# Down products reading their operand at other addresses, and an up product in halves of 256 columns

## The chip, the cores and the metric

The kernel runs on one core of one Trainium2 chip. The metric is the device time of one execution in microseconds. Matrix products run on TensorE (PE in the rows; PEld is its weight load), the rest on VectorE (DVE), ScalarE (ACT) and GpSimd (POOL); SyncE (SP) issues the weights' DMAs.

## The reference

Two layers on a sequence of 512 tokens of width 1024. Layer 1 mixes with a convolution and a recurrence, layer 2 with sliding-window attention. Each layer ends in the same feed-forward block, and that block is all that the change touches:

```
def conv_glu_ffn(x, norm_g, w_up, conv_w, conv_b, w_down):      # D_FF = 2816
    h = rms_norm(x, norm_g)
    u = h @ w_up                                                # [512,1024] @ [1024,5632]
    gate = causal_dwconv(u[..., :D_FF], conv_w, conv_b)         # 3 taps
    return (jax.nn.silu(gate) * u[..., D_FF:]) @ w_down         # [512,2816] @ [2816,1024]
```

## The kernel before, in words

Everything lies feature-major: 128 features on the partitions, the 512 tokens as columns. A product of float32 exactness is made of three products of rounded halves (type float32r): weights and operand are each split into a high and a low part, and for each 128x128 block of weights TensorE does high weights by high operand, high by low, low by high. That is `gemm` (lines 167 to 178). Each of the three is one MATMUL of 128x512 with a weight load of 128x128 of its own in front of it, so the high weights are loaded twice.

`wpieces` and `wparts` (lines 143 to 164) bring the weights: a raw piece of 128x1024 by one DMA on SP's queue (two buffers), of which ScalarE casts one half at a time to `whi` (line 150) and VectorE subtracts to `wlo` (line 151). `whi` and `wlo` have three buffers each (WHL = 3). One such half feeds two output blocks by two blocks of depth, so 12 MATMULs.

`ffn` (line 680) runs eleven rounds over pairs of feature blocks. A round has two up products: `pg` for the gate and `pu` for the other factor, 48 MATMULs each, with `xgh` and `xgl` as the moving operand. Then VectorE scales the gate (`gp`, line 707), ScalarE and VectorE apply the taps (lines 709 and 712), ScalarE the silu, VectorE multiplies by `pu` (line 715), and the result is split into row f of `hh` and `hl` (lines 183 and 184). After the rounds the down product reads `hh` and `hl` as its moving operand: eight output blocks by 22 blocks of depth by 3 parts, 528 MATMULs. The order of the instructions on each engine is written by the program's scheduler from the dependences; TensorE takes its MATMULs in the order in which they stand.

Where the operands lie in a partition (bytes, from the built program of before; all rows of an operand are 2048 bytes apart, all blocks of weights 512 bytes):

```
operand                  first byte          the same modulo 512   product that reads it
whi, wlo (all buffers)   78912 ... 89152      64                   every product (weights)
xgh, xgl                 37952, 54336         64                   up products, keys, queries
oh, ol                   139904, 156288      128                   attention's output (lines 174, bank)
mc, mr                   121280, 137664      448                   mixer's output (lines 174, bank)
hh, hl (both layers)     104800, 149856      352                   down products
```

The attention's value product (line 866) is the one place where a float32r product already streams 256 columns at a time: there `xgh` or `xgl` is the loaded operand (128x128) and `whi` or `wlo` the moving one, as two runs of 128 columns, 2048 bytes apart.

Of the kernel before, what the change touches and what calls it, by code (L numbers as in the profile page):

```python
# [11 lines left out]
F32 = mybir.dt.float32  # L12
F32R = mybir.dt.float32r
# [4 lines left out]
DRAM = bass.MemoryType.DRAM  # L18

P = 128  # L20
T = 512
D = 1024
# [12 lines left out]
FC = DFF // P  # L35
# [21 lines left out]
# vectors of the features, in columns of 128: widths in columns, first columns  # L57
# [11 lines left out]
class Net:  # L69
# [17 lines left out]
    # activations that share a table set, in the order of the sets  # L87
# [17 lines left out]
    # banks: rings of one pool; those of the large products in turn, those of everything else in turn  # L105
# [60 lines left out]
    # m blocks of the product, over the blocks kb..ke of its depth; xh, xl start at block kb  # L166
    def gemm(self, w, b0, xh, xl, m=2, kb=0, ke=None, pss=None, first=True, last=True, prep=None):
        ke = w.shape[2] if ke is None else ke
        pss = pss or [self.pmm() for _ in range(m)]
        for k0, kn, hi, lo in self.wpieces(w, b0, m, kb, ke, prep):  # L170
            for i, ps in enumerate(pss):
                for k in range(kn):
                    kk = k0 + k - kb
                    mm = lambda a, b, **kw: self.nc.tensor.matmul(ps, lhsT=a[:, i, k, :], rhs=b[:, kk, :], **kw)  # L174
                    mm(hi, xh, start=first and kk == 0, stop=False)
                    mm(hi, xl, start=False, stop=False)
                    mm(lo, xh, start=False, stop=last and k0 + k == ke - 1)
        return pss
# [12 lines left out]
    # rs = rsqrt(-2 * ps + eps), ps = -0.5 * mean square  # L191
# [14 lines left out]
    # residual stream -> gained and split operand of the next product, and its rms factor  # L206
# [48 lines left out]
    def mixer(self):  # L255
        nc, tc, ap = self.nc, self.tc, self.ap
        V, S, G = nc.vector, nc.scalar, nc.gpsimd
# [5 lines left out]
        with ExitStack() as es:  # L263
# [70 lines left out]
            # mt: rows (S | k), columns (a t | r t); mbt: b rows (r t), and the transposed inverses;  # L334
            # bkt, sv: token-major (b | k) decayed to the chunk end, and (S | v)
# [21 lines left out]
            def keys(fc):  # L357
# [4 lines left out]
                # normalised key (negated)  # L362
# [30 lines left out]
                # in-chunk matrices, transposed: rows (b s | k s), columns (a t | r t)  # L393
# [15 lines left out]
                # the corner between the two diagonal blocks waits in the room of the states  # L409
                S.copy(sv[0:LH, fc, :, :, 0:LH], mt[0:LH, :, :, LH:L])  # L410
                S.copy(mbt[0:64, fc], mt[0:64, :, :, L:P])
                # the rows of b have left; the chunk-start features take their place
                for eo in range(2):
                    G.dma_start(mt[0:64, eo], ar[eo * 64 : eo * 64 + 64])
                # bonus: the decays of r and of k cancel
# [12 lines left out]
            def values(fc):  # L428
                bk, ep = bks[fc], eps[fc]
                v = shift(self.gemm(win, 16 + fc, xh, xl, m=1)[0], 8 + fc, "v")  # L430
                V.tensor_tensor(out=bv[:, fc, :], in0=bv[:, fc, :], in1=v, op=ALU.mult)
                # token-major b, k (decayed to the chunk end) and v
                for c in range(NCH):
                    S.activation(out=bk[:, c, :], in_=bk[:, c, :], func=AF.Identity, scale=ep[:, c, L : L + 1])
                for c0 in range(0, NCH, 4):
                    p4 = self.psum().rearrange("p (c t) -> p c t", t=P)
                    for c in range(4):
                        nc.tensor.transpose(out=p4[:, c, :], in_=bk[:, c0 + c, :], identity=self.ident)
                    S.copy(bkt[:, fc, :, c0 : c0 + 4, :].rearrange("p e c n -> p c e n"), p4.rearrange("p c (e n) -> p c e n", e=2))
                    p4 = self.psum().rearrange("p (c t) -> p c t", t=P)  # L440
                    for c in range(4):
                        cc = c0 + c
                        if cc == 0:
                            nc.tensor.matmul(p4[64:128, c, :], lhsT=v[:, 0:L], rhs=self.ident, start=True, stop=True)
                        else:
                            nc.tensor.transpose(out=p4[:, c, :], in_=v[:, (cc - 1) * L : (cc + 1) * L], identity=self.ident)
                    S.copy(sv[64:128, fc, :, c0 : c0 + 4, :].rearrange("p e c n -> p c e n"),
                           p4[64:128].rearrange("p c (e n) -> p c e n", e=2))

# [81 lines left out]
            for c in range(NCH):  # L531
                for g in range(2):
# [8 lines left out]
                    # four products are open at once in this bank: products with zeros open and close them all  # L541
# [12 lines left out]
                    # the updates take the place of the state  # L554
# [124 lines left out]
    def ffn(self, l, out=None, aside=None):  # L679
# [7 lines left out]
        with ExitStack() as es:  # L687
# [3 lines left out]
            hh = big.tile([P, FC, T], F32R, name="hh")  # L691
            hl = big.tile([P, FC, T], F32R, name="hl")
            rstd = big.tile([P, T], F32, name="rstd")
            for fp in range(FC // 2):
                if fp == 2 and aside:
                    aside()
                pg = self.gemm(wu, 2 * fp, xh, xl)
                if fp == 0:
                    self.table("natural_log_exp_and_others")
                    self.rms_rows(tr, "t2", rstd, ln=True)  # L700
                    self.table("silu_and_others")
                pu = self.gemm(wu, FC + 2 * fp, xh, xl)
                for i in range(2):
                    f = 2 * fp + i
                    gp = tr.tile([P, 2 + T], F32, tag="gp", name="gp")
                    G.memset(gp[:, 0:2], 0.0)  # L706
                    V.tensor_tensor(out=gp[:, 2:], in0=pg[i], in1=rstd, op=ALU.mult)  # L707
                    t = tr.tile([P, T], F32, tag="t2", name="t", bufs=T3)
                    S.activation(out=t, in_=gp[:, 2:], func=AF.Identity, scale=self.pc("ffn_conv_w", (3 * l + 2) * FC + f),  # L709
                                 bias=self.pc("ffn_conv_b", l * FC + f))  # L710
                    for j in (1, 0):
                        V.scalar_tensor_tensor(out=t, in0=gp[:, j : j + T], scalar=self.pc("ffn_conv_w", (3 * l + j) * FC + f), in1=t,  # L712
                                               op0=ALU.mult, op1=ALU.add)
                    self.fn(out=t, in_=t, func=AF.Silu)
                    V.tensor_tensor(out=t, in0=t, in1=pu[i], op=ALU.mult)  # L715
                    self.split(hh[:, f, :], hl[:, f, :], t)
            for b0 in range(0, DC, 2):
                for i, ps in enumerate(self.gemm(wd, b0, hh, hl)):
                    m = b0 + i
# [76 lines left out]
    def attention(self):  # L796
# [10 lines left out]
        with ExitStack() as es:  # L807
# [24 lines left out]
            # keys: normalised, rotated, on both halves of the partitions  # L832
# [25 lines left out]
            # values, token-major  # L858
# [14 lines left out]
            # queries: biased, gained, rotated; the rms factor waits for the scores  # L873
# [3 lines left out]
            def queries(j):  # L877
# [9 lines left out]
                # -(rms factor) / 8  # L887
# [14 lines left out]
            def block(m, b):  # L902
# [8 lines left out]
                # row tiles of the tensor engine run side by side: even and odd heads on two banks  # L911
# [21 lines left out]
                for kb in range(nkb):  # L933
# [3 lines left out]
                    # even heads first  # L937
# [39 lines left out]
def _blocks(w):  # L977
    # [K, M] -> [M / 128, 128 (row in block), K / 128, 128 (column in block)]
    k, m = w.shape
    return w.reshape(k // P, P, m // P, P).transpose(2, 1, 0, 3)  # L980


def _columns(inputs):
# [5 lines left out]
    # conv taps: rows (tap mod 4, channel mod 32), columns (channel / 32, tap / 4)  # L989
# [40 lines left out]
```

## Time and profile before

| | us |
|---|---|
| three timed executions | 1236.13, 1236.25, 1239.99 |
| median | 1236.25 |
| span of the profiled execution, first to last instruction | 1235.5 |
| TensorE busy | 1216.2 (98% of the span), 6231 MATMULs, 6231 weight loads |
| VectorE, ScalarE busy | 717.7 (58%), 551.1 (45%) |
| granted TensorE clock, mean | 0.999 |
| layer 1: up product, down product (from, to) | 359.7 to 555.7 (last nine rounds), 555.7 to 678.9 |
| layer 2: up product, down product (from, to) | 867.1 to 1107.3, 1107.3 to 1230.2 |

The profile gives no time of the profiled execution beside its span; the span lies 0.75 us under the median of the timed runs. A MATMUL's length in the profile is from its start until its result is out, and consecutive ones overlap. What a MATMUL costs in a stream is the distance from its start to the next one's start.

### The profile page before, as it was taken

Reading aid. Unit: us, or ns where it says so; the run is one execution under the profiler, and the core shown is the slowest. Engines: PE = TensorE matmul, PEld = TensorE weight load, DVE = VectorE, ACT = ScalarE, POOL = GpSimd, SP = SyncE. Lnnn points to the kernel's source line nnn. Section 1 sums busy time; section 2 is a strip of 40 time slices with the busy share of each in tenths; the row PEclk is TensorE's granted clock in tenths of the full one; section 3 lists DMA queues with packets and bytes.
Section 4 is the critical chain, followed back from the end, with each engine's and each line's share of the span. In section 5 each row is a group of like instructions: output and inputs, shape, how many; then the busy total and the mean of one; then the engine's idle time right before and its main releaser. Section 6 shows DMA issues by size and latency. Waiting matters only on the chain.

```text
span 1235.5 us, 16559 instructions
## 1 busy us (share of the span) xinstructions
PE 1216.2 (98%) x6231; PEld 948.3 (77%) x6231; DVE 717.7 (58%) x1360; ACT 551.1 (45%) x1031; POOL 72.0 (6%) x210
## 2 busy tenths in 40 slices
PE   7999999999999999999999999999999999999998
PEld 5687875568788888888888876658888888888886
DVE  6797947367766555553333678866655455553332
ACT  6967333365534343342222657764544343432221
POOL 4101031000100000000000030100000000000000
PEclk9999999999999999999999999999999999999999
DMA  6235382022323322323333230102223223233331
GB/s 188 57 90 128 94 196 59 1 86 93 96 98 102 103 88 101 102 87 95 94 95 97 85 103 25 55 20 100 89 99 102 93 96 103 94 94 111 111 111 60
DMA packets 65088, 114.42 MB, mean 93 GB/s; under 512 B 15681, under 2 KB 17937, under 8 KB 65009
## 3 DMA queue, kind: packets, MB, share of 16 engines
q1 hardware_dynamic: 60048, 102.25, 26.9%
q0 software_dynamic: 4816, 10.89, 3.5%
q8 instruction: 49, 0.80, 0.3%
q14 instruction: 31, 0.25, 0.1%
q10 hardware_dynamic: 144, 0.23, 0.1%
HBM read 105.40 MB, written 4.26 MB: 89 GB/s over the span
## 4 chain that ended last, share of the span: by engine, by line
PE 93%; DVE 3%; ACT 2%; DMA 2%; issue 1%; SPq 0%; ACTq 0%; DVEq 0%
PE mm L174 66%; PE bank L174 11%; PE mm L631 2%; PE bank L917 2%; PE bank L942 2%; PE bank L936 1%; PE ps L404 1%; DMA xT<-in_xT_dram 1%; PE ps L538 1%; PE ps L553 1%; PE ps L559 1%; PE bank L885 1%; DMA nb<-nd 1%; PE ps L567 0%; DVE wlo L151 0%
## 5 line engine op out<-in xcount | busy, mean ns | idle before, releaser
L151 DVE TENSOR_TENSOR wlo<-wraw,whi 128x512 fp32r<-128x512 f32 x364 | 250.8, 690 | 360.5 <-ACT whi L150 353.2
L150 ACT CAST whi<-wraw 128x512 fp32r<-128x512 f32 x364 | 224.8, 618 | 431.2 <-PE mm L174 374.9
L174 PE MATMUL mm<-xgh,whi 128*128 128x512 f32 x896 | 351.6, 392 | 9.9 <-ACT whi L150 9.9
L174 PE MATMUL mm<-xgh,wlo 128*128 128x512 f32 x896 | 350.4, 391 | 0.2 <-DVE wlo L151 0.2
L174 PE MATMUL mm<-xgl,whi 128*128 128x512 f32 x896 | 350.2, 391 | 0.0
L174 PEld LDWEIGHTS mm<-xgh,whi 128*128 128x128 f32 x896 | 168.6, 188 | 47.2 <-ACT whi L150 10.1
L174 PEld LDWEIGHTS mm<-xgh,wlo 128*128 128x128 f32 x896 | 168.5, 188 | 37.8 <-issue 1.7
L174 PEld LDWEIGHTS mm<-xgl,whi 128*128 128x128 f32 x896 | 168.6, 188 | 36.1 <-issue 1.2
L174 PE MATMUL mm<-hh,whi 128*128 128x512 f32 x352 | 139.1, 395 | 0.0
L174 PE MATMUL mm<-hh,wlo 128*128 128x512 f32 x352 | 139.0, 395 | 0.0
L174 PE MATMUL mm<-hl,whi 128*128 128x512 f32 x352 | 139.0, 395 | 0.0
L174 PEld LDWEIGHTS mm<-hh,wlo 128*128 128x128 f32 x352 | 66.0, 187 | 16.3
L174 PEld LDWEIGHTS mm<-hl,whi 128*128 128x128 f32 x352 | 66.0, 187 | 16.1
L174 PEld LDWEIGHTS mm<-hh,whi 128*128 128x128 f32 x352 | 66.0, 187 | 16.0
L712 DVE SCALAR_TENSOR_TENSOR t<-gp,col,t 128x512 f32<-128x512 f32 x88 | 63.5, 745 | 0.0
L709 ACT ACTIVATE t<-gp,col 128x512 f32<-128x512 f32 x44 | 35.7, 816 | 35.3 <-DVE gp L707 34.7
L183 ACT CAST hh<-t 128x512 fp32r<-128x512 f32 x44 | 27.3, 622 | 36.9 <-DVE t L715 36.6
L707 DVE TENSOR_TENSOR gp<-mm,rstd 128x512 f32<-128x512 f32 x44 | 30.2, 691 | 17.3 <-PE mm L174 17.2
L715 DVE TENSOR_TENSOR t<-t,mm 128x512 f32<-128x512 f32 x44 | 30.1, 687 | 17.2 <-PE mm L174 17.2
L101 ACT ACTIVATE t<-t 128x512 f32<-128x512 f32 x44 | 27.7, 630 | 20.4 <-DVE t L712 20.3
L706 POOL MEMSET gp<- 128x2 f32 x44 | 4.5, 105 | 512.3 <-DVE t L712 451.5
L922 DVE CUSTOM_DVE_ANT_0 pr<-bank,mask,nsnk 128x256 f32<-128x256 f32 (+1 forms) x64 | 31.3, 502 | 3.8 <-PE bank L917 3.7
(323 smaller groups left out, 1452.9 us busy)
## 6 DMA issues: line engine op xcount, KB each, us to landing
wraw<-in_w_up_dram SPq DMA_DIRECT2D x88, 512.0 KB, 3.5
wraw<-in_w_down_dram SPq DMA_DIRECT2D x40, 512.0 KB, 3.7
wraw<-in_w_in_dram SPq DMA_DIRECT2D x22, 512.0 KB, 3.7
wraw<-in_w_qkv_dram SPq DMA_DIRECT2D x12, 512.0 KB, 3.5
wraw<-in_w_out_dram SPq DMA_DIRECT2D x8, 512.0 KB, 3.6
wraw<-in_w_o_dram SPq DMA_DIRECT2D x8, 512.0 KB, 3.5
st<-cpad POOLq DMA_DIRECT2D x24, 135.0 KB, 4.6
xT<-in_xT_dram SPq DMA_DIRECT2D x4, 512.0 KB, 8.6
```

Of the source, the lines that this page charges most:

```text
L101: ins = self.nc.scalar.activation(**kw)
L150: nc.scalar.copy(hi, src)
L151: nc.vector.tensor_tensor(out=lo, in0=src, in1=hi.bitcast(F32), op=ALU.subtract)
L174: mm = lambda a, b, **kw: self.nc.tensor.matmul(ps, lhsT=a[:, i, k, :], rhs=b[:, kk, :], **kw)
L183: nc.scalar.copy(hi, src)
L631: nc.tensor.matmul(pc[b * 32 : b * 32 + 32, :], lhsT=dg[:, b, g, :], rhs=stk[b][:, 4 * g : 4 * g + T], start=g == 0, stop=g == 7, tile_pos ...
L707: V.tensor_tensor(out=gp[:, 2:], in0=pg[i], in1=rstd, op=ALU.mult)
L709: S.activation(out=t, in_=gp[:, 2:], func=AF.Identity, scale=self.pc("ffn_conv_w", (3 * l + 2) * FC + f), bias=self.pc("ffn_conv_b", l * F ...
L712: V.scalar_tensor_tensor(out=t, in0=gp[:, j : j + T], scalar=self.pc("ffn_conv_w", (3 * l + j) * FC + f), in1=t, op0=ALU.mult, op1=ALU.add)
L715: V.tensor_tensor(out=t, in0=t, in1=pu[i], op=ALU.mult)
L917: nc.tensor.matmul(pscs[e][:, hp, :nk], lhsT=qr[hs, h // 2, bs], rhs=kd[m][hs, k0 : k0 + nk], start=True, stop=True)
L922: V.tensor_tensor_reduce(out=pr_[:, i, :nk], in0=pscs[e][:, hp, :nk], in1=mask[:, 2 * P - nk :], op0=ALU.add, op1=ALU.min, scale=rq[:, b, ...
```

## The change

- `gemm` has a new argument `parts`. With 2, each block's three products are done for columns 0 to 255 first and then for columns 256 to 511, each with a weight load of its own. Layer 2's up products have `parts=2`; all others stay at 1.
- Layer 1: a tile of 224 bytes that nobody uses stands ahead of `hh`. In the built program `hh` and `hl` move from 104800 and 149856 to 105024 and 150080, both 64 modulo 512, as the weights.
- Layer 2: rows of `hh` and `hl` are 2080 bytes apart in place of 2048. They begin at 104800 and 150560, and row k lies at 352 + 32 k and 32 + 32 k modulo 512.
- Comments are dropped, which moves line numbers (174 becomes 176, 712 becomes 719).

```
-    def gemm(self, w, b0, xh, xl, ..., prep=None):
+    def gemm(self, w, b0, xh, xl, ..., prep=None, parts=1):
...
-                    mm = lambda a, b, **kw: self.nc.tensor.matmul(ps, lhsT=a[:, i, k, :], rhs=b[:, kk, :], **kw)
-                    mm(hi, xh, start=first and kk == 0, stop=False)
-                    mm(hi, xl, start=False, stop=False)
-                    mm(lo, xh, start=False, stop=last and k0 + k == ke - 1)
+                    for c in range(parts):
+                        cs = slice(c * T // parts, (c + 1) * T // parts)
+                        mm = lambda a, b, **kw: self.nc.tensor.matmul(ps[:, cs], lhsT=a[:, i, k, :], rhs=b[:, kk, cs], **kw)
+                        mm(hi, xh, start=first and kk == 0 and c == 0, stop=False)
+                        mm(hi, xl, start=False, stop=False)
+                        mm(lo, xh, start=False, stop=last and k0 + k == ke - 1 and c == parts - 1)
...
-            hh = big.tile([P, FC, T], F32R, name="hh")
-            hl = big.tile([P, FC, T], F32R, name="hl")
+            if l == 0:
+                big.tile([P, 56], F32, name="gap")
+                hh = big.tile([P, FC, T], F32R, name="hh")
+                hl = big.tile([P, FC, T], F32R, name="hl")
+            else:
+                hh = big.tile([P, FC, T + 8], F32R, name="hh")[:, :, 0:T]
+                hl = big.tile([P, FC, T + 8], F32R, name="hl")[:, :, 0:T]
...
-                pg = self.gemm(wu, 2 * fp, xh, xl)
+                pg = self.gemm(wu, 2 * fp, xh, xl, parts=1 + l)
...
-                pu = self.gemm(wu, FC + 2 * fp, xh, xl)
+                pu = self.gemm(wu, FC + 2 * fp, xh, xl, parts=1 + l)
```

TensorE, where layer 2's up product begins, before (`mm` is an output bank, `xgh` and `xgl` the operand's parts, `whi` and `wlo` the weights'; the number after a name is its buffer):

```order
L174 MATMUL mm_7386<-xgh_7359,whi_7390 128x512
L174 MATMUL mm_7386<-xgl_7360,whi_7390 128x512
L174 MATMUL mm_7386<-xgh_7359,wlo_7391 128x512
L174 MATMUL mm_7386<-xgh_7359,whi_7390 128x512
L174 MATMUL mm_7386<-xgl_7360,whi_7390 128x512
L174 MATMUL mm_7386<-xgh_7359,wlo_7391 128x512
```

The same place in the changed kernel:

```order
L176 MATMUL mm_7387<-xgh_7360,whi_7391 128x256
L176 MATMUL mm_7387<-xgl_7361,whi_7391 128x256
L176 MATMUL mm_7387<-xgh_7360,wlo_7392 128x256
L176 MATMUL mm_7387<-xgh_7360,whi_7391 128x256
L176 MATMUL mm_7387<-xgl_7361,whi_7391 128x256
L176 MATMUL mm_7387<-xgh_7360,wlo_7392 128x256
L176 MATMUL mm_7387<-xgh_7360,whi_7391 128x256
L176 MATMUL mm_7387<-xgl_7361,whi_7391 128x256
L176 MATMUL mm_7387<-xgh_7360,wlo_7392 128x256
L176 MATMUL mm_7387<-xgh_7360,whi_7391 128x256
L176 MATMUL mm_7387<-xgl_7361,whi_7391 128x256
L176 MATMUL mm_7387<-xgh_7360,wlo_7392 128x256
```

Six MATMULs of 512 columns became twelve of 256; TensorE has 1056 instructions more of this kind over the stage (22 products of 48), and as many weight loads, and nothing else on it moves.

VectorE in one round of layer 2's up product, before (`gp` is the scaled gate, the SCALAR_TENSOR_TENSOR rows are the taps):

```order
L707 TENSOR_TENSOR gp<-mm,rstd 128x512 x2
L712 SCALAR_TENSOR_TENSOR t<-gp,col,t 128x512
L151 TENSOR_TENSOR wlo<-wraw,whi 128x512
L712 SCALAR_TENSOR_TENSOR t<-gp,col,t 128x512 x2
L151 TENSOR_TENSOR wlo<-wraw,whi 128x512
L712 SCALAR_TENSOR_TENSOR t<-gp,col,t 128x512
L151 TENSOR_TENSOR wlo<-wraw,whi 128x512 x2
L715 TENSOR_TENSOR t<-t,mm 128x512 x2
```

The same round in the changed kernel:

```order
L714 TENSOR_TENSOR gp<-mm,rstd 128x512 x2
L151 TENSOR_TENSOR wlo<-wraw,whi 128x512
L719 SCALAR_TENSOR_TENSOR t<-gp,col,t 128x512 x4
L151 TENSOR_TENSOR wlo<-wraw,whi 128x512 x3
L722 TENSOR_TENSOR t<-t,mm 128x512
L186 TENSOR_TENSOR hl<-t,hh 128x512
L722 TENSOR_TENSOR t<-t,mm 128x512
```

The scheduler put the four taps together, so one subtraction for the weights now stands behind all four instead of between them; the number of instructions on VectorE is the same. ScalarE, GpSimd and the DMA queues keep their order.

## Rows read from the trace of the kernel before

**Rows 1.** The page: busy time, granted clock by fortieths, the chain of waits by engine.
```profile
PE 1216.2 (98%) x6231; PEld 948.3 (77%) x6231; DVE 717.7 (58%) x1360; ACT 551.1 (45%) x1031; POOL 72.0 (6%) x210
...
PEclk9999999999999999999999999999999999999999
...
PE 93%; DVE 3%; ACT 2%; DMA 2%; issue 1%; SPq 0%; ACTq 0%; DVEq 0%
```

**Rows 2.** The chain of waits in order: start us, us, engine, tile, line, count.
```profile
281.74 29.07 PE bank L174 x125
...
359.85 330.11 PE mm L174 x1440
...
830.87 36.23 PE bank L174 x157
...
878.89 351.75 PE mm L174 x1536
```

**Rows 3.** Busy time by stretch: from:to, length, each engine, clock, DMA share, GB/s.
```profile
555.70:678.80 123.10, 123.10 (x529) 98.91 (x528) 45.01 (x67) 31.96 (x52) 0.00 (x0) 1.00 0.33 94
867.10:1107.20 240.10, 240.10 (x1059) 198.40 (x1058) 133.51 (x203) 100.96 (x161) 2.01 (x20) 1.00 0.29 97
1107.30:1230.20 122.90, 122.90 (x528) 98.74 (x527) 39.47 (x59) 26.85 (x44) 0.00 (x0) 1.00 0.34 99
```

**Rows 4.** Groups in layer 2's up product: busy, mean ns, idle before, releaser.
```profile
L174 PE MATMUL mm<-xgh,whi 128*128 128x512 f32 x352 | 137.4, 390 | 0.0
...
L151 DVE TENSOR_TENSOR wlo<-wraw,whi 128x512 fp32r<-128x512 f32 x88 | 60.7, 690 | 86.0 <-ACT whi L150 86.0
...
L712 DVE SCALAR_TENSOR_TENSOR t<-gp,col,t 128x512 f32<-128x512 f32 x44 | 31.7, 745 | 0.0
```

**Rows 5.** TensorE in order of time, up product: start us, us, instruction.
```profile
419.68 0.39 PE L174 MATMUL mm<-xgh,whi 128*128 128x512 f32 x1
...
427.84 0.39 PE L174 MATMUL mm<-xgh,whi 128*128 128x512 f32 x1
```

**Rows 6.** The same view, layer 1's down product.
```profile
639.68 0.39 PE L174 MATMUL mm<-hh,whi 128*128 128x512 f32 x1
...
649.95 0.39 PE L174 MATMUL mm<-hh,wlo 128*128 128x512 f32 x1
```

**Rows 7.** The same view, the attention's value product, with weight loads (PEld).
```profile
691.01 0.28 PE L866 MATMUL mm<-whi,xgh 128*128 128x256 f32 x1
691.02 0.19 PEld L866 LDWEIGHTS mm<-wlo,xgh 128*128 128x128 f32 x1
...
694.49 0.28 PE L866 MATMUL mm<-whi,xgl 128*128 128x256 f32 x1
```

**Rows 8.** The same view, eight transposes of 128 columns in the attention.
```profile
744.50 1.04 PE L936 MATMUL bank<-ident,pr 128*128 128x128 f32 x8
```

**Rows 9.** Groups of TensorE by shape over the whole span.
```profile
L936 PE MATMUL bank<-ident,pr 128*128 128x128 f32 x112 | 18.9, 280 | 0.1
```

**Rows 10.** ScalarE in a round of layer 2's up product, in order of time.
```profile
963.07 0.62 ACT L150 CAST whi<-wraw 128x512 fp32r<-128x512 f32 x1 [2.05 <-PE mm L174]
...
966.11 0.60 ACT L150 CAST whi<-wraw 128x512 fp32r<-128x512 f32 x1
966.75 0.81 ACT L709 ACTIVATE t<-gp,col 128x512 f32<-128x512 f32 x1
968.57 0.62 ACT L150 CAST whi<-wraw 128x512 fp32r<-128x512 f32 x1 [1.00 <-PE mm L174]
```

More of the change, by code (lines that the diff above doesn't have):

```diff
@@ L164, in wpieces, with gemm @@
                 yield p0 + k0, kn, hi, lo
-    def gemm(self, w, b0, xh, xl, m=2, kb=0, ke=None, pss=None, first=True, last=True, prep=None):
+    def gemm(self, w, b0, xh, xl, m=2, kb=0, ke=None, pss=None, first=True, last=True, prep=None, parts=1):
         ke = w.shape[2] if ke is None else ke
```

## The prediction

> **What bounds the kernel now.** I read the page first: TensorE is busy for 98% of the span, the clock is granted in full, and the chain that ended last is TensorE's for 93% [rows 1]. Then the chain in order of time. It holds two long unbroken pieces of MATMULs, 330.11 us with 1440 of them and 351.75 us with 1536, and layer 2's feed-forward is the second of these, down to the end of the program [rows 2]. The table by stretch says the same: in layer 2's up and down products, and layer 1's down product, TensorE is busy for the whole stretch [rows 3]. In the up product no MATMUL waited (0.0 idle), and ScalarE and VectorE wait for TensorE's buffers instead [rows 4, 10]. So a nanosecond per MATMUL in these stages is on the path, and no edit elsewhere is.
>
> What a MATMUL costs is then the distance between starts. Up product: from 419.68 to 427.84 are 36 steps, 226.7 ns each [rows 5]. Down product: from 639.68 to 649.95 are 44 steps, 233.4 ns [rows 6]. Value product, 256 columns: from 691.01 to 694.49 are 29 steps, 120.0 ns [rows 7]. The long piece of the chain checks the first two: 1008 up MATMULs by 226.7 and 528 down ones by 233.4 are 351.7 us, against 351.75 [rows 2].
>
> [...]
>
> **The change part by part.**
>
> *Layer 2's up product in halves.* It has 22 products of 48, so 1056 MATMULs of 512 columns, which become 2112 of 256. [...] The nearest row is the value product, 120.0 ns, same number of columns, float32r, a 128x128 load each, both operands at 64 modulo 512 [rows 7]; the second half begins 1024 bytes further on, again at 64. I take 120.0. A pair costs 240.0 against 226.7, and 1056 times 13.3 ns is **+14.0 us** (bounds 0 and +28.4). The loads don't become the limit: eight transposes that load 128 columns each take 1.04 us, of which one is 0.28 long, so seven steps take 0.76 us, 109 ns each, under 120 [rows 8, 9].
>
> [...]
>
> *The other engines in that stage.* VectorE's order moves: one subtraction for `wlo` now stands behind four taps. Three buffers hide it. In the old round the cast at 966.11 came when a piece was freed; TensorE has two more pieces of 12 MATMULs, 2 x 2.72 = 5.4 us, before it needs the result. The cast takes 0.62 us and the subtraction 0.69 [rows 4, 10], leaving some 4.1 us. The second pair of taps waits for ScalarE until 967.56 (966.75 + 0.81), four taps take at most 3.0 us (745 ns each), and the next subtraction, whose cast ends at 969.2, is done by about 971.3. It is needed at 968.57 + 5.4 = 974.0 and two MATMULs more. That leaves 2.7 us, and halves give it 0.3 us more. Cost 0; with the cover gone, each of ten rounds would wait for what is missing. The raw weights' DMA is paced by the same pieces, now slower, and costs 0.
>
> *Layer 1's down product at the weights' phase.* 528 MATMULs. Operand and weights then stand to each other as in the up product (both 64 modulo 512). Bounds: no change, or the up product's 226.7 in place of 233.4. I take the second, because it is the same combination: 528 x 6.7 ns = **-3.5 us** (bounds 0 and -3.5).
>
> *Layer 2's down product with rows of 2080 bytes.* Row k of `hh` lies at 352 + 32 k and row k of `hl` at 32 + 32 k modulo 512, so 22 rows run through all sixteen places 32 bytes apart, and the weights stay at 64. The trace has four places. Distance 0: 226.7. Distance 288: 233.4. Distance 384 (the mixer's output): 29.07 us for 125, 232.6. Distance 64 (the attention's output): 36.23 us for 157, 230.8 [rows 2, 5, 6]. The last two hold a few steps that are long for other reasons, so they are upper ends. All sixteen places in turn should give something between the ends, and I take the middle of 226.7 and 233.4, 230.0 ns: 528 x 3.4 ns = **-1.8 us**. Bounds: -3.5 if nearly every row is as good as distance 0; +3.5 if places that the trace doesn't show are as much worse than 288 as 0 is better.
>
> [...]
>
> *Elsewhere.* Places of later tiles in the feed-forward's pools move too. Those are read by VectorE and ScalarE only, which wait for TensorE there. Cost 0. At the end of the program the last two multiplications and additions stay as they are.
>
> Sum: +14.0 - 3.5 - 1.8 = +8.7 us. The profiled span is 1235.5, the forecast span 1244.2, and with the 0.75 us between span and median (1236.25) the time is **1245.0 us**.
>
> **The rivals.**
>
> *A half costs half* (the other side: faster). The value product's moving operand is two runs of 128 columns that lie 2048 bytes apart. If its excess came from the step between runs rather than from the load, one run of 256 would take 113.3 ns and the split would be free. For it: the form does differ [rows 7]. [...] The time: 1236.25 - 5.3 = 1231.0. It decides below 115.9 ns for a half, where twice the half less 226.7 is 5.3 us / 1056 = 5.0 ns. [...]
>
> *Addresses don't matter.* The down products' excess has another cause (their depth, their place in the program) and only the split counts: 1236.25 + 14.0 = 1250.3. For it: no row shows a down product at another address, and distances 64 and 384 lie close to 288. Against: stages are alike in all else, and the excess is the same in both layers (123.10 and 122.90 us for the stage [rows 3]). [...]
>
> *VectorE is late.* With the taps together, `wlo` misses its time, and TensorE waits about 1 us in each of ten rounds on top of the forecast: 1255. Against: the 2.7 us above. It decides when the subtraction ends more than 2.7 us later than reckoned.
>
> **How the numbers follow.** Forecast 0.75, addresses without effect 0.11, a half costs half 0.08, VectorE late 0.03, and 0.03 for a mix in which a half falls between 114 and 117 ns. A measurement of this kernel tells about 0.3% from no change, 3.7 us: faster is under 1232.5, slower over 1240. The forecast with its own ends is 1241 to 1249 (the layer 2 addresses give -1.7 to +5.3 about it, a half 119 to 121 ns gives 2 us either way, and layer 1 at most +3.5); the range of 8 in 10 takes in the addresses' rival and stops short of the free split: 1240 to 1251. Faster: most of the free split, 0.06. Within 0.3%: the rest of it and the mix, 0.06. Slower: 0.88.
>
> **What would show it.** In the changed profile: 7287 weight loads in place of 6231; starts 120 ns apart in layer 2's up product and the stage at some 254 us in place of 240; starts 226.7 ns apart in layer 1's down product (119.7 us in place of 123.1); about 230 in layer 2's, varying from row to row with the operand's place; no idle of TensorE behind VectorE's `wlo`. The forecast is wrong if the halves start under 116 ns apart, if layer 1's down product keeps 233 ns, or if rows of layer 2's down product go beyond 233.

## The result, and the profile after

The changed kernel takes 1247.09 us (median of four executions, 1246.54 to 1247.48), the kernel before 1236.88 (median of four, 1236.13 to 1239.99). The ratio is 1.0076 with a 95% interval of 1.0064 to 1.0089: slower by 0.8%. Forecast were 1245.0 us, in a range from 1240 to 1251.

TensorE still bounds. From the page of the changed kernel, to be read beside [rows 1]:

```profile
PE 1226.6 (98%) x7287; PEld 1004.2 (81%) x7287; DVE 719.1 (58%) x1360; ACT 551.8 (44%) x1031; POOL 72.0 (6%) x210
...
PE 93%; DVE 3%; ACT 2%; DMA 1%; issue 1%; SPq 0%; ACTq 0%; DVEq 0%
```

There are 1056 MATMULs and weight loads more, and the shares of the chain are as they were, but for DMA (1% in place of 2%). Next the chain of waits in order of time, with the same columns as [rows 2]:

```profile
281.90 29.17 PE bank L176 x125
...
360.11 326.55 PE mm L176 x1440
...
827.70 36.24 PE bank L176 x157
...
876.32 364.59 PE mm L176 x2544
```

The reader sees the whole result in two rows. The piece with layer 1's up and down product is 3.56 us shorter (330.11 before), the piece with layer 2's 12.84 us longer (351.75), and the other two are within 0.1 us of before. (The last piece starts after the first of the 22 up products, so it holds most of the stage's change, not all.) Then the table by stretch, layer 1's down product, layer 2's up and layer 2's down (columns as [rows 3]):

```profile
556.00:675.60 119.60, 119.60 (x529) 99.07 (x528) 44.92 (x67) 31.80 (x53) 0.00 (x0) 1.00 0.34 97
863.80:1118.00 254.20, 254.20 (x2115) 253.72 (x2114) 134.84 (x203) 102.25 (x161) 1.98 (x20) 1.00 0.29 92
1118.10:1240.50 122.40, 122.40 (x529) 98.90 (x528) 39.59 (x59) 26.72 (x44) 0.00 (x0) 1.00 0.33 99
```

From the first start of a stage to the first start after it, layer 1's down product takes 119.68 us in place of 123.20 (-3.5). Layer 2's up product takes 254.28 in place of 240.32 (+14.0, from the end of the attention's output product on). The rest of the span is 127.66 in place of 128.21 (-0.5). These sum to +9.9 of the span's +10.2 us; 0.3 us come elsewhere, where nothing differs.

TensorE in order of time in layer 2's up product (14 steps in 1.68 us, 120.0 ns each, against [rows 5]):

```profile
899.78 0.28 PE L176 MATMUL mm<-xgh,wlo 128*128 128x256 f32 x1
...
901.46 0.28 PE L176 MATMUL mm<-xgl,whi 128*128 128x256 f32 x1
```

And in layer 1's down product (38 steps in 8.61 us, 226.6 ns each, against [rows 6]):

```profile
599.68 0.39 PE L176 MATMUL mm<-hl,whi 128*128 128x512 f32 x1
...
608.29 0.39 PE L176 MATMUL mm<-hh,whi 128*128 128x512 f32 x1
```

The groups of layer 2's up product, columns as [rows 4]: no idle time stands before TensorE's MATMULs (0.0).

```profile
L176 PE MATMUL mm<-xgh,whi 128*128 128x256 f32 x704 | 199.6, 284 | 0.0
...
L176 PEld LDWEIGHTS mm<-xgh,wlo 128*128 128x128 f32 x704 | 135.2, 192 | 0.0
```

VectorE in the new order, in one round of that product (start us, us, instruction):

```profile
969.14 0.69 DVE L151 TENSOR_TENSOR wlo<-wraw,whi 128x512 fp32r<-128x512 f32 x1
969.75 2.73 DVE L719 SCALAR_TENSOR_TENSOR t<-gp,col,t 128x512 f32<-128x512 f32 x4
972.40 0.69 DVE L151 TENSOR_TENSOR wlo<-wraw,whi 128x512 fp32r<-128x512 f32 x1
```

and ScalarE's cast for the last of these:

```profile
971.31 0.62 ACT L150 CAST whi<-wraw 128x512 fp32r<-128x512 f32 x1 [1.27 <-PE mm L176]
```

The cast ends at 971.93 and its subtraction starts at 972.40. The four taps in a row made it 0.5 us late. It ends at 973.09, and TensorE needs it two pieces of 24 halves (5.8 us) after the cast began, at about 977.1, so 4 us are left.

### The profile page after: what moved, and what is told of

The parts are those of the page before. It is cut to its first block, busy times and chain, and to the rows that moved or that the text cites. A ratio compares the mean times of both kernels' runs of the same rounds, so it can differ in the third digit from the quotient of the medians.

```text
span 1245.7 us, 18672 instructions
## 1 busy us (share of the span) xinstructions
PE 1226.6 (98%) x7287; PEld 1004.2 (81%) x7287; DVE 719.1 (58%) x1360; ACT 551.8 (44%) x1031; POOL 72.0 (6%) x210
## 4 chain that ended last, share of the span: by engine, by line
PE 93%; DVE 3%; ACT 2%; DMA 1%; issue 1%; SPq 0%; ACTq 0%; DVEq 0%
PE mm L176 67%; PE bank L176 11%; PE mm L633 2%; PE bank L924 2%; PE bank L949 2%; PE bank L943 1%; PE ps L406 1%; PE ps L540 1%; PE ps L555 1%; PE ps L561 1%; DMA nb<-nd 1%; PE bank L892 1%; PE ps L569 0%; PE ps L548 0%; DVE wlo L151 0%
## 5 line engine op out<-in xcount | busy, mean ns | idle before, releaser
L176 PE MATMUL mm<-xgh,whi 128*128 128x256 f32 (+1 forms) x1248 | 413.9, 332 | 9.4 <-ACT whi L150 9.4
L176 PE MATMUL mm<-xgh,wlo 128*128 128x256 f32 (+1 forms) x1248 | 412.9, 331 | 0.0
L176 PE MATMUL mm<-xgl,whi 128*128 128x256 f32 (+1 forms) x1248 | 412.6, 331 | 0.0
L176 PEld LDWEIGHTS mm<-xgh,whi 128*128 128x128 f32 x1248 | 237.8, 191 | 33.0 <-ACT whi L150 8.3
L176 PEld LDWEIGHTS mm<-xgh,wlo 128*128 128x128 f32 x1248 | 237.7, 190 | 23.6 <-issue 1.7
L176 PEld LDWEIGHTS mm<-xgl,whi 128*128 128x128 f32 x1248 | 237.9, 191 | 22.4 <-issue 1.2
L722 DVE TENSOR_TENSOR t<-t,mm 128x512 f32<-128x512 f32 x44 | 30.1, 686 | 10.3 <-PE mm L176 10.2
L186 DVE TENSOR_TENSOR hl<-t,hh 128x512 fp32r<-128x512 f32 x44 | 30.1, 688 | 7.7 <-ACT hh L185 6.9
```

The lines of the kernel that those rows point to most:

```text
L176: mm = lambda a, b, **kw: self.nc.tensor.matmul(ps[:, cs], lhsT=a[:, i, k, :], rhs=b[:, kk, cs], **kw)
L186: nc.vector.tensor_tensor(out=lo, in0=src, in1=hi.bitcast(F32), op=ALU.subtract)
```

## The experiments

Twelve kernels ran. All are the changed kernel with other numbers in the three places; two have further gaps, ahead of the mixer's and the attention's tiles or of the weights. A step below is the distance between starts, from the first start of a stage to its last, divided by the number of steps. The two large rows of the chain, shown for most runs, agree with it within 0.1 ns: 233.3 ns plus a 528th of the difference to the row of before [rows 2], and half of that for a half. Distance means operand minus weights, in bytes modulo 512. The ratios of the first four are to fifteen executions of the kernel before (median 1236.72 us). The other eight kernels ran once each, and their steps are read rather than their times.

**The halves alone.** `hh` and `hl` as before.

```
-                hh = big.tile([P, FC, T + 8], F32R, name="hh")[:, :, 0:T]
+                hh = big.tile([P, FC, T], F32R, name="hh")       # hl alike, no gap tile
```

> The changed kernel with hh and hl where they were before; only layer 2's up products go in halves. Theory (every MATMUL pays 13.3 ns beside its columns, whatever its length): layer 2's up stage 254.3 us in place of 240.1, both down products 123.2 and 123.0 as before, span 1235.5 + 14.1 = 1249.6. Rival (the stage is longer for another reason that came with the moved operand, such as VectorE's new places): the up stage shorter than 254.

Measured 1253.66 us (1250.01 to 1254.17, four executions), ratio 1.0129 (1.0116 to 1.0143). Layer 2's up product by stretch:

```profile
869.30:1123.40 254.10, 254.10 (x2115) 253.62 (x2114) 134.89 (x203) 102.19 (x161) 2.00 (x20) 1.00 0.28 92
```

The stage is the theory's 254.3 us, from 869.2 to 1123.5, and both down products are as before. So the places of the operand in the changed kernel add nothing to the up product. The span is 1251.7, 2.1 more than expected. Its chain has that in the mixer, ahead of all that differs:

```profile
112.95 8.26 DMA nb<-nd
121.50 0.66 DVE v L322
...
133.55 41.07 PE mm L176 x181
```

The last row starts at 131.44 in the changed kernel and at 130.7 to 132.8 in the other runs. The DMA is one of the mixer's round trips; what follows it starts at 121.50, against 120.49 in the changed kernel, so about half of the 2.1 us is there by the DMA's end and the rest comes between there and 133.55. Three of four executions were about as long as this one; only this one was traced, and why is open.

**Both down products at distance 0, no halves.**

```
-            if l == 0:
-                big.tile([P, 56], F32, name="gap")
+            big.tile([P, 56], F32, name="gap")                  # both layers, all parts=1
```

> No halves; hh and hl of both layers begin at 64 modulo 512, as the weights. Theory (distance of operand to weights modulo 512 sets the step, 0 gives 226.7 ns): both down products 119.7 us, span 1235.5 - 3.5 - 3.3 = 1228.7, about 0.55% faster. Rival (layer 1's gain came with its place in the program): layer 2's stays at 123.

Measured 1230.22 us (1229.07 to 1231.26, five executions), ratio 0.9947 (0.9934 to 0.9959). The chain's two rows:

```profile
359.62 326.55 PE mm L176 x1440
...
875.12 348.22 PE mm L176 x1536
```

They are 3.56 and 3.53 us shorter: both layers do 226.7 ns a step. The rival, that layer 1's gain came with its place in the program, falls.

**Mixer's and attention's output products at distance 0 too.**

```
+            big.tile([P, 32], F32, name="gap_m")                # ahead of the mixer's big tiles
+            cst.tile([P, 112], F32, name="gap_a")               # ahead of oh, ol
```

> As phase_both, and also oh, ol (attention's output product) and mc, mr (mixer's output product) at 64 modulo 512. Theory: 192 MATMULs of each product go from about 230.8 and 232.6 to near 227 ns, another 0.7 and 1.1 us off: span about 1226.9. Rival (those products are long for interruptions, not for places): the same as phase_both, 1228.7.

Measured 1228.40 us (1228.26 to 1229.21, five executions), ratio 0.9933 (0.9920 to 0.9945): the best version here, faster than both kernels. The mixer's and the attention's rows:

```profile
281.10 31.32 PE bank L176 x138
...
825.83 35.91 PE bank L176 x157
```

The attention's row is 0.32 us shorter (36.23), the mixer's 0.76 (32.08 in runs whose chain also has 138 of them). Theory gave 0.7 and 1.1 for 192 MATMULs; the rows hold 157 and 138. Scaled to 192 by count, an estimate, they make 0.4 and 1.1: the mixer's gain is the theory's, the attention's falls short. Its steps that nothing interrupts went from 229.0 to 227.1 ns (the mixer's from 232.4 to 226.8). The theory's 230.8 had two long steps and the row's end in it, so there the rival is right in part.

**Rows of 2080 bytes in layer 2 alone.**

```
+            w = T + (8 if l else 0)
+            hh = big.tile([P, FC, w], F32R, name="hh")[:, :, 0:T]     # hl alike
```

> Only layer 2's rows of 2080 bytes. Theory (each row costs what its place costs, and nearly all places but distance 0 cost 231 to 235 ns): layer 2's down product 122.4 us as in the changed kernel, span 1235.0, not to be told from before by time. Rival (the changed kernel's 122.4 depends on what the up product in halves left behind): another length of the stage.

Measured 1236.67 us (ten executions, 1235.33 to 1237.62) against 1236.72, ratio 0.9996 (0.9987 to 1.0005). The chain's last long row:

```profile
879.53 351.20 PE mm L176 x1536
```

It is 0.55 us shorter, a step of 232.3 ns, in the changed kernel too. This edit alone is worth half a microsecond.

**The weights moved by 32 bytes**, so that the distance changes in every product over `xgh` and `xgl`, which stay where they are. Operands that lie behind the weights move along.

```
+        pool(name="padw", bufs=1).tile([P, 8], F32, name="padw")      # ahead of the weights' pool
+            gap = (56, 48)[l]
```

> No halves; the weights' buffers lie 32 bytes further on, at 96 modulo 512. Layer 1's hh, hl at 96 (distance 0), layer 2's at 64 (distance 480), xgh and xgl stay at 64 (distance 480). Theory (the distance between operand and weights counts): layer 1's down product 119.7 us, layer 2's about 123 (233 ns a step), and the up products rise from 226.7 to about 233 ns, layer 1's nine rounds from 196.0 to some 201.5 us, layer 2's alike: span about 1235 - 3.5 + 12 = 1244. Rival (the operand's own place counts, 64-byte boundary good, 32 off it bad): layer 1's down 123.2, layer 2's down 119.7, up products unchanged, span 1232. Second rival (both have to lie on 64-byte boundaries): all of them near 233.

Measured 1249.21 us, one execution. Layer 1's up and down product and layer 2's by stretch:

```profile
362.00:563.60 201.60, 201.60 (x865) 162.37 (x866) 115.25 (x179) 81.13 (x131) 1.78 (x16) 1.00 0.28 94
563.70:683.30 119.60, 119.60 (x529) 99.07 (x528) 44.88 (x67) 31.72 (x52) 0.00 (x0) 1.00 0.33 97
872.10:1119.20 247.10, 247.10 (x1059) 198.69 (x1058) 134.23 (x203) 101.00 (x161) 1.98 (x20) 1.00 0.28 94
1119.30:1242.20 122.90, 122.90 (x528) 98.97 (x527) 39.55 (x59) 26.75 (x44) 0.00 (x0) 1.00 0.33 98
```

The up products got longer (196.0 to 201.7 and 240.3 to 247.2 us; 226.7 to 233.3 ns a step) although neither their operand nor their instructions changed, and layer 1's down product, 32 bytes off a 64-byte boundary like its weights, is at its best. Layer 2's, on a 64-byte boundary with weights off it, stays at 233.3. Both rivals fall: the distance counts. The span of 1247.4 is 3.4 us over the forecast 1244; 2.1 of them are other products over `xgh` (1.16 us and 0.91 us in the mixer) that were left out of it.

The same run moves the value product's weights, which are its moving operand, to 32 bytes beyond its loaded operand modulo 512 (0 before), and leaves its two runs of 128 columns as they are. Before, it took 120.0 ns [rows 7]; here 31 steps take 3.62 us, 116.8 ns each (and 117.8 over the second group of 42 steps):

```profile
695.53 0.28 PE L872 MATMUL mm<-wlo,xgh 128*128 128x256 f32 x1
...
699.15 0.28 PE L872 MATMUL mm<-whi,xgl 128*128 128x256 f32 x1
```

**Constant distances.** Four runs with a gap of other sizes, no halves; one layer each.

```
+            gap = (72, 120)[l]      # distances 64 and 256; (88, 104): 128, 192; (80, 96): 96, 160
+            o = (4, 0)[l]           # 16 bytes, by a slice; with gap (56, 64): 16 and 32
```

> No halves; layer 1's hh, hl at distance 64 from the weights (modulo 512), layer 2's at 256, same for all rows. Theory (each place has its price, and rows of 2080 bytes gained little because all places but 0 are dear): distance 64 near 229 to 231 ns (121 to 122 us for the stage), 256 near 231 (122 us). Rival (places are cheap by themselves, going from row to row with the place changing is what costs): both at 227 to 228 ns, 119.7 to 120.4 us.

```profile
361.28 327.79 PE mm L176 x1440
...
878.06 348.22 PE mm L176 x1536
```

Distance 64: 228.9 ns, as expected. Distance 256: 226.7, not 231: as good as 0, so between these two distances the step repeats after 256 bytes.

> No halves; layer 1's hh, hl at distance 16 from the weights, layer 2's at 32, same for all rows. How sharp is distance 0? Theory of a sharp place: 16 and 32 both at 231 to 235 ns (122 to 124 us). Rival (the step rises with the distance): 227 ns at 16, 227.5 at 32, under 120.2 us.

```profile
360.08 329.22 PE mm L176 x1440
...
878.20 351.75 PE mm L176 x1536
```

231.7 ns at 16 and 233.3 at 32: the good place is sharp. The rival falls.

> Whole MATMULs of 512 columns, down products at distances 128 (layer 1) and 192 (layer 2). Known: 0 and 256 give 226.7, 16: 231.7, 32, 288 and 480: 233.4, 64: 228.9. Theory (period 256, dear off the 64-byte grid, dearer the farther on it): 128 some 229 to 232, 192 as 64. Rival (period 128): 128 gives 226.7 and 192 gives 228.9: stages 119.7 and 120.9 us.

```profile
359.78 330.08 PE mm L176 x1440
...
878.82 351.74 PE mm L176 x1536
```

Both 233.3 ns. So 128 bytes is not the period, and 192 is no mirror of 64; theory and rival were wrong at both places.

> Whole MATMULs, down products at distances 96 (layer 1) and 160 (layer 2), the two multiples of 32 below 256 that are not yet measured. Theory (rows of 2080 bytes cost the mean of their places): with 233.3 ns at both, the eight places average 231.9 ns, against 232.3 measured for those rows; stages 123.2 us each. Rival (going from row to row costs by itself): if 96 and 160 are cheaper, 229 ns or less, the places' mean is under 230.9 and 1.4 ns a step are left to the changes of place.

```profile
360.40 330.12 PE mm L176 x1440
...
879.41 352.23 PE mm L176 x1536
```

233.4 and 234.3 ns. With these the eight multiples of 32 below 256 are known (224 from the moved weights). Their mean is 232.1 ns, against 232.3 for rows that run through them. The places account for the rows' price; 0.2 ns at most are left to going from place to place.

**Halves in the down products.**

```
-                for i, ps in enumerate(self.gemm(wd, b0, hh, hl)):
+                for i, ps in enumerate(self.gemm(wd, b0, hh, hl, parts=1 + l)):     # then parts=2
```

> No moved operands; layer 2's down product (distance 288) in halves of 256 columns, its up product whole. [...] Rival (13.3 ns come with the load, the 6.7 of the bad place with the columns): 123.4 ns a half, stage 130.3 us, span +7.3.

```profile
879.01 351.74 PE mm L176 x2064
```

1056 halves take what 528 whole MATMULs took (351.74 us in this row, 351.75 before): 116.7 ns a half, 233.3 a pair, at distance 288. Halving is free there. The rival falls, and so does the price of distance 0 carried over whole: the value product's 120.0 ns and the 6.7 by which a whole is dearer here make 126.7 a half, an estimate from [rows 5], [rows 6] and [rows 7].

> Both down products in halves of 256 columns, up products whole; hh, hl at distance 0 from the weights (modulo 512) in layer 1, at 192 in layer 2. The halves at distance 288 cost 116.7 ns, nothing over half of the whole 233.3. Theory (the place sets the price of halving too, and at distance 0 it is 13.3 ns a pair): layer 1's down product at 120.0 ns a half, 126.7 us. Rival (the down product, by its depth or buffers, halves for free, the up product doesn't): 113.3 ns, 119.7 us. Layer 2 at 192: between 113.3 and 120 ns; not known better.

```profile
360.26 333.61 PE mm L176 x1968
...
882.80 352.92 PE mm L176 x2064
```

At distance 0 a half takes 120.0 ns: the product is 3.50 us longer than before, and 7.06 longer than with whole MATMULs at the same place (326.55, in the run of both down products at distance 0). So it is the place and not the product that sets the price of halving. At 192 a half costs 117.8.

> Both down products in halves, at distances 64 (layer 1) and 128 (layer 2). Theory (place alone): 64 between the 120.0 of distance 0 and the 116.7 of distance 288, and a pair not under the whole MATMUL's 228.9, so 121 to 127 us. Is any pair under the whole's best, 226.7? If a half falls under 113.3 ns, halving would gain at that place; expected: no.

```profile
359.54 331.29 PE mm L176 x1968
...
879.85 355.25 PE mm L176 x2064
```

117.8 ns at 64 and 120.0 at 128; the theory's range for 64 (121 to 127 us) holds with 124.4, though a half at 64 is nearer to the cheapest than to that of distance 0. No pair comes under the whole's best, 226.7.

## Why the prediction was right, point by point

*What bounds.* Right. In every run the span moved by the step of a MATMUL times their number, to within 1.5 us, but for the run with the halves alone, whose mixer was 2.1 us longer.

*Layer 2's up product in halves: +14.0.* The number is exact (+13.96 measured, 120.0 ns a half), the reason given for it, that every MATMUL pays 13.3 ns beside its columns at whatever length, too wide. At distance 0 the steps fit it: a whole takes 226.7 ns and a half 120.0, so 256 columns more take 106.7, which leaves 13.3 of the half. That these come with the load was the author's estimate; no run times columns without a load. At 288 a whole takes 233.3 and a half 116.7, so nothing is left, and halving costs nothing. The number could be carried over from the value product because it, too, stands at distance 0, which the prediction did name as a likeness; the same reason, tried at distance 288, gave 126.7 ns a half, where 116.7 was measured. The upper bound, +28.4 us, rests on a time of columns without a load that no run shows; the dearest half measured took 120.0 ns, and a half at the down product's place 116.7. The loads' limit did not bind: loads cover 253.72 of 254.20 us of the stage, but 116.7 ns a half with as many loads was reached elsewhere.

*VectorE's order: 0.* Right; 0.5 us late, hidden.

*Layer 1 at the weights' phase: -3.5.* Right in size (-3.52) and reason. The moved weights show that it is the distance.

*Layer 2's rows of 2080 bytes: -1.8.* This term was mis-sized: -0.55 measured, inside its bounds. The step that failed is the middle of 226.7 and 233.4 for "all sixteen places". Only 0 and 256 are good, 64 costs 228.9, 16 231.7, and all other multiples of 32 are at 233.3 to 234.3. The values in the trace for other places were read as upper ends of something lower. For 64 that was so (230.8 against 228.9); for 384, the same as 128, the 232.6 was the price itself: the steps of that product that nothing interrupts take 232.4 ns before and 233.3 in the changed kernel (why they differ at the same place is open). One of the prediction's signs of being wrong also came, in small: rows go beyond 233. In the changed kernel's trace the mean step of a row (24 MATMULs) runs from 230.3 to 234.2 ns, and rows held at 160 take 234.3.

*From span to time.* The prediction put 0.75 us between span and time, from a median of other executions. Each run since lists both for the same execution, and the time is 1.8 us over the span in all (1247.48 and 1245.7; 1228.29 and 1226.5; 1253.51 and 1251.7). If that held for the profiled execution of before, it took about 1237.3, and the same sum would have given 1246.0. This 1.0 us, 1.25 us of the rows and 0.3 us elsewhere make up the 2.5 us between forecast and profiled execution.

*The sums.* One doesn't come out as written. The forecast's own ends (-1.7 and -2 below; +5.3, +2 and +3.5 above) make 1241 below, but 1256 above in place of 1249, so the upper end of the range rests on judgement.

*The rivals.* "A half costs half" is wrong at distance 0 (120.0 ns, where half of a whole is 113.3); at 288 a half costs half of the whole at that place (116.7 of 233.3). That rival blamed the two runs of the value product's operand for the 6.7 ns above half; the place was the cause, since the same two runs took 116.8 to 117.8 ns once the weights had moved. "Addresses don't matter", which put the 6.7 ns of a down product's step above an up product's down to another cause, is contradicted by the moved weights: the same streams slowed by 6.6 ns a step (226.7 to 233.3).

## What to carry to other kernels

Where TensorE streams 512 columns of float32r back to back with a load for each MATMUL, as here, place the moving operand at distance 0 or 256 from the blocks of weights (226.7 ns a step, against 228.9 to 234.3 at the other distances measured), and give every row the same place. Here that is a gap tile of 224 bytes in each layer, worth 6.5 us of 1236.7; in layer 2, rows of 2080 bytes (232.3 ns a step) brought 0.55 us of the 3.53. Other types were not tried, and for halves of 256 columns the cheapest place measured was another (116.7 ns at 288, 120.0 at 0). Take a price for a new shape from a row at the same place: halving cost 13.3 ns a pair at distance 0 and nothing at 288.

## What the hardware showed that was not expected

Steps in ns (granted clock 0.999 to 1.000 over each profiled run). "-" was not run. At distance 0 a whole takes 106.7 ns more than a half, for 256 columns more, and at 32 it takes 116.6 more.

```
distance (mod 256)     0      16     32     64     96     128    160    192    224
whole, 512 columns     226.7  231.7  233.3  228.9  233.4  233.3  234.3  233.3  233.3
half, 256 columns      120.0  -      116.7  117.8  -      120.0  -      117.8  -
two halves - whole     13.3   -      0      6.6    -      6.7    -      2.2    -
```

Wholes were run at 0 and 256, and at 32 and 288, with equal results; the repeat after 256 bytes rests on these two pairs; the halves in column 32 were run at 288, and the value product, its moving operand 32 bytes beyond the loaded one, came to 116.8 and 117.8. The best place for a whole is among the worst for a half (226.7 and 120.0 at 0). Moving the weights took the up products' step from 226.7 to 233.3, and moving the operand took the down products' from 233.3 to 226.7, so here the step goes with where the two stand to each other. Why it does, and why halving costs 13.3 ns a pair at 0 and nothing at 32, no run here tells.
